# A hybrid decoder step on one core: PSUM banks and the token shift's way out of PSUM

## Chip, cores and metric

One core of a Trainium2 chip. The metric is the device time of one execution in microseconds, the median of the runs; lower is better. The kernel holds its numbers in fp32; a dense product is three passes of a rounded high part and a low part.

## What is computed

One layer over 1024 prompt tokens and 8 x 4 sample tokens (1056 columns in all), cut to what matters:

```
h = rmsnorm(x) ; z = h @ w_in                       # conv | r,k,v,lora | gates
xs = zr + (prev(zr) - zr) * mu                      # token shift: one token back
r, k, v, decay, alr, gout = from xs (three small lora products)
S_t = S_{t-1} diag(w_t) + (S_{t-1} a_t) b_t^T + v_t k_t^T ;  y_t = S_t r_t   # 16 heads, 64 x 64
y = groupnorm(y) ... ; ya = conv branch ; x += (sigmoid(zg0) * ya + sigmoid(zg1) * (y @ w_rw_out)) @ w_mix_out
x += (gelu(conv3(h2 @ w_up)[:half]) * conv3(...)[half:]) @ w_down ; rmsnorm
```

Outputs are the activations and the new conv, shift, wkv and ffn states.

## The kernel before

A dense product makes one tile of 128 output channels: `project_g` (L75) runs three blocks of 352 tokens, each 8 x 3 matmuls into one PSUM bank of the pool `pm` (tag mm, three banks), and hands each finished block to an eviction function. The weight tile comes by DMA, ScalarE rounds it (`whi`, L48), GpSimd makes the rest (`wlo`, L49).

The program has four parts. `load_in` and `norm_in` load and normalize. `mixer_a` does the conv tiles with their 31 taps on VectorE (L359), the lora products and the r, k, v tiles of the first two column groups. `mixer_b` runs the recurrence. `tail` does the merge, the output product and the feed-forward part with PSUM pools of its own.

In `mixer_b` the recurrence is cut into 16 pieces (4 groups of 4 heads, 4 quarters of the prompt), each of four chunks of 64 tokens. Nine generators, the streams, are recorded together with the dense tiles by `drive` (L701): a stream step that is due by an estimated tensor-engine clock is recorded, else one step of a dense tile, the fillers: first 18 tiles of r, k, v with their token shift, then 16 gate tiles, then 8 conv output tiles once the last chain is done. The streams are: `prep` (decays, normalized keys, the bonus; L885), `stage` (in-chunk products, L992, and a triangular solve of 31 steps on VectorE, L1026 to L1030, whose tiles go by DMA through DRAM), `combine` (L1061), `chain` (L1089: four steps, each a product from the state, a copy R0, a product, a scaled write of U, a product, the new state), `group_norm` (L1159), the samples' streams, the layer norm of the conv branch, and the shift output. They take working tiles from a pool of `T2N` = 12 buffers through a counter (`take`, L730).

From this record a scheduler sets the order on each engine; an engine then works strictly in it. PSUM has eight banks: three for dense tiles (tag mm), two that all streams share (tag w, `pw_tile`, L879), and one each for the chain (c), its output (y) and the solve (x). The same pools serve the first stages.

The token shift (`shifted`, L481) empties a dense bank in these steps: ScalarE writes (1 - mu) times the block (L490), VectorE adds mu times the block, one column to the right, reading PSUM (L492), adds the column kept from the block before (`bcol`, L494), keeps the last column (L496), and in the last block handles the samples and copies the shift state (`shcol`, L502, L503).

Of the kernel before, what the change touches and what calls it, by code (L numbers as in the profile page):

```python
# [7 lines left out]
F32 = mybir.dt.float32  # L8
# [3 lines left out]
ALU = mybir.AluOpType  # L12
# [19 lines left out]
class Net:  # L32
# [68 lines left out]
    def build(self):  # L101
        with ExitStack() as es:
# [6 lines left out]
            with ExitStack() as e1:  # L109
                self.rp = self.pool(e1, "wraw", 1)  # L110
                with ExitStack() as e:
                    self.pm = self.pool(e1, "pm", 3, space=PSUM)
                    self.pw = self.pool(e1, "pw", 2, space=PSUM)
                    xs, w0 = self.load_in(e)
                    self.norm_in(e, xs)
                with ExitStack() as e:
                    self.t4 = self.pool(e, "t4", 8)
                    self.mixer_a(w0)
                self.mixer_b()
# [132 lines left out]
    def mixer_a(self, w0):  # L252
# [5 lines left out]
        self.bcol = self.cp.tile([128, NSH, 2], F32, name="bcol")  # L258
# [128 lines left out]
    def ln_block(self, b):  # L387
# [14 lines left out]
        ps = self.pw_tile()  # L402
# [5 lines left out]
        ps = self.pw_tile()  # L408
# [72 lines left out]
    def shifted(self, w, j, out, m=128):  # L481
# [3 lines left out]
        bc = self.bcol[:m, j]  # L485
        add = lambda o, i: nc.vector.scalar_tensor_tensor(out=o, in0=i, scalar=mu, in1=o, op0=ALU.mult, op1=ALU.add)  # L486

        def ev(b, s, ps):
            t0 = b * BW
            nc.scalar.activation(out=out[:m, s], in_=ps, func=AF.Copy, scale=om)  # L490
            n = min(TP - t0, BW)
            add(out[:m, t0 + 1:t0 + n], ps[:, 0:n - 1])  # L492
            if b:
                add(out[:m, t0:t0 + 1], bc[:, b - 1:b])  # L494
            if n == BW:
                nc.vector.tensor_copy(out=bc[:, b:b + 1], in_=ps[:, n - 1:n])  # L496
            else:
                x = out[:m, TP:T].rearrange("p (b t) -> p b t", t=4)
                z = ps[:, n:BW].rearrange("p (b t) -> p b t", t=4)
                add(x[:, :, 1:4], z[:, :, 0:3])  # L500
                add(x[:, :, 0], self.shT[:m, j])
                nc.vector.tensor_copy(out=self.shcol[:m, j, 0:1], in_=ps[:, n - 1:n])  # L502
                nc.vector.tensor_copy(out=self.shcol[:m, j, 1:9], in_=z[:, :, 3])  # L503
# [165 lines left out]
    T2N = 12  # L669
# [157 lines left out]
    def s_shift(self):  # L827
# [3 lines left out]
        for g in range(7):  # L831
            yield from self.take(1)
            ps = self.pw_tile()
# [45 lines left out]
    def pw_tile(self):  # L879
        return self.pw.tile([128, 512], F32, tag="w", name="w")  # L880

# [3 lines left out]
    def prep(self, n):  # L885
# [79 lines left out]
        for u in ([slice(0, 1), slice(1, 2)] if smp else [slice(0, 2)]):  # L965
            ps = self.pw_tile()
# [715 lines left out]
```

## Time and profile before

| | us |
|---|---|
| median of 3 runs | 2560.39 (2559.02 to 2569.0) |
| profiled execution | 2538.03 |
| its span, first to last instruction | 2536.3 |
| tensor engine (PE) busy | 2367.6 |
| VectorE (DVE) busy | 1427.9 |
| ScalarE (ACT) busy | 918.7 |
| GpSimd (POOL) busy | 909.1 |

The engines' times overlap. Matmuls are pipelined, so a busy PE is not one at its peak. PEclk is the granted share of the tensor engine's full clock. PEld is the weight load, SP the engine that issues DMAs. A line such as L486 is a line of the kernel before; where a helper records an operation, the line is the helper's (L54 is every matmul, L61 every transpose of the recurrence). In the changed kernel the lines stand 4 to 17 further down.

### The profile page before, as it was taken

The numbers are of one execution on the slowest core, as the hardware profiler recorded it, in microseconds if no ns is written. First come the engines' busy times: TensorE is split into PE (matmuls) and PEld (weight loads), VectorE is DVE, ScalarE is ACT, GpSimd is POOL, SyncE is SP. The second block draws the span as 40 slices with busy tenths as digits, with TensorE's granted clock in tenths as the row PEclk, the third lists the DMA queues.
The fourth block names the chain that finished last, engine by engine and source line by source line (L and its number), as shares of the span: only waits on it lengthen the run. The fifth ranks groups of instructions, "written<-read, shape, count | busy, mean of one in ns | idle before, by whom it ended". The sixth has DMA issues, their size and how long they took to land.

```text
span 2536.3 us, 41660 instructions
## 1 busy us (share of the span) xinstructions
PE 2367.6 (93%) x16094; PEld 2140.9 (84%) x16094; DVE 1427.9 (56%) x3588; ACT 918.7 (36%) x1748; POOL 909.1 (36%) x879
## 2 busy tenths in 40 slices
PE   5889989999788799999989999999999999999998
PEld 4878888777676677777777899999999999999998
DVE  5799955586646674555464434465444534445345
ACT  4133433354244354454434322333222222223125
POOL 3332253244324443443333243433323323323333
PEclk9899987898688698999779999999999999999999
DMA  3223443243233333533323854431111111111111
GB/s 104 56 60 130 171 149 89 81 121 93 78 89 79 93 107 83 140 98 94 94 64 96 273 178 131 128 128 44 44 47 48 44 51 44 47 48 41 54 46 75
DMA packets 307640, 230.64 MB, mean 91 GB/s; under 512 B 90492, under 2 KB 287123, under 8 KB 306921
## 3 DMA queue, kind: packets, MB, share of 16 engines
q1 hardware_dynamic: 307185, 227.80, 31.1%
q8 instruction: 127, 2.08, 0.4%
q14 instruction: 72, 0.59, 0.1%
q0 software_dynamic: 256, 0.17, 0.0%
HBM read 157.45 MB, written 70.45 MB: 90 GB/s over the span
## 4 chain that ended last, share of the span: by engine, by line
PE 66%; DVE 7%; DMA 7%; POOL 3%; issue 2%; ACT 1%; SPq 1%; POOLq 0%; DVEq 0%; ACTq 0%
PE mm L54 52%; PE w L54 7%; DMA L<-dL 4%; PE c L54 2%; PE y L54 2%; PE w L61 2%; DVE tm L1028 1%; DVE x L1030 1%; DVE t L961 1%; DMA ga<-d_ga 0%; POOL BK L982 0%; POOL wlo L49 0%; POOL LQ L1011 0%; DVE lnQ L666 0%; DVE v L486 0%
## 5 line engine op out<-in xcount | busy, mean ns | idle before, releaser
L54 PE MATMUL mm<-hH,whi 128*128 128x352 f32 (+1 forms) x2568 | 887.6, 346 | 27.0 <-DVE bcol L496 11.2
L54 PE MATMUL mm<-hL,whi 128*128 128x352 f32 (+1 forms) x2568 | 866.2, 337 | 0.2 <-DVE hL L248 0.2
L54 PE MATMUL mm<-hH,wlo 128*128 128x352 f32 (+1 forms) x2568 | 862.7, 336 | 0.0
L54 PEld LDWEIGHTS mm<-hH,whi 128*128 128x128 f32 (+1 forms) x2568 | 499.4, 194 | 55.9 <-issue 14.1
L54 PEld LDWEIGHTS mm<-hL,whi 128*128 128x128 f32 (+1 forms) x2568 | 500.9, 195 | 11.2 <-DVE hL L248 0.5
L54 PEld LDWEIGHTS mm<-hH,wlo 128*128 128x128 f32 (+1 forms) x2568 | 500.6, 195 | 8.7 <-issue 0.2
L49 POOL TENSOR_TENSOR wlo<-wraw,whi 128x1024 fp32r<-128x1024 f32 (+2 forms) x123 | 292.5, 2378 | 462.0 <-ACT whi L48 427.9
L48 ACT ACTIVATE whi<-wraw 128x1024 fp32r<-128x1024 f32 (+2 forms) x123 | 126.0, 1025 | 366.8 <-PE mm L54 270.1
L1544 DVE SCALAR_TENSOR_TENSOR c<-u,par,c 128x1024 f32<-128x1024 f32 x96 | 167.0, 1739 | 55.6 <-ACT c L1540 55.6
L359 DVE SCALAR_TENSOR_TENSOR sg<-cu,par,sg 128x1024 f32<-128x1024 f32 x120 | 185.1, 1550 | 3.4 <-ACT sg L357 1.7
L1514 DVE TENSOR_TENSOR u<-mm,rs 128x352 f32<-128x352 f32 x144 | 73.2, 509 | 186.5 <-PE mm L54 186.3
L54 PE MATMUL mm<-fH,whi 128*128 128x352 f32 x504 | 163.4, 324 | 0.0
L1569 DVE TENSOR_TENSOR acc<-mm,acc 128x352 f32<-128x352 f32 x168 | 86.8, 523 | 135.0 <-PE mm L54 135.0
L54 PE MATMUL mm<-fH,wlo 128*128 128x352 f32 x504 | 162.7, 323 | 0.0
L54 PE MATMUL mm<-fL,whi 128*128 128x352 f32 x504 | 162.7, 323 | 0.0
L1028 DVE TENSOR_TENSOR tm<-L,x 128x60 f32<-128x60 f32 (+24 forms) x496 | 99.4, 200 | 79.7 <-DMA L<-dL 72.5
L1030 DVE TENSOR_TENSOR x<-x,tm 128x60 f32<-128x60 f32 (+24 forms) x496 | 105.0, 212 | 7.0
L1525 POOL COPY lr<-u 128x2 f32<-128x2 f32 x48 | 9.0, 187 | 276.3 <-DVE u L1514 267.6
L54 PE MATMUL w<-E,BK 64*128 64x128 f32 x512 | 90.7, 337 | 8.8 <-DVE tm L1028 3.4
L1011 POOL TENSOR_SCALAR_AFFINE_SELECT LQ<-LQ 64x512 f32<-64x512 f32 x64 | 44.1, 690 | 148.3 <-ACT LQ L1007 146.8
L54 PEld LDWEIGHTS mm<-fH,whi 128*128 128x128 f32 x504 | 94.8, 188 | 0.5
L54 PEld LDWEIGHTS mm<-fH,wlo 128*128 128x128 f32 x504 | 95.0, 188 | 0.0
(379 smaller groups left out, 3971.2 us busy)
## 6 DMA issues: line engine op xcount, KB each, us to landing
wraw<-w_in SPq DMA_DIRECT2D x50, 512.0 KB
wraw<-w_up SPq DMA_DIRECT2D x48, 512.0 KB
wraw<-w_down SPq DMA_DIRECT2D x32, 384.0 KB
L<-dL SPq DMA_DIRECT2D x16, 512.0 KB
d_alr<-la SPq DMA_DIRECT2D x8, 528.0 KB
d_cum<-lc SPq DMA_DIRECT2D x8, 528.0 KB
d_gout<-lg SPq DMA_DIRECT2D x8, 528.0 KB
d_k<-k SPq DMA_DIRECT2D x8, 528.0 KB
```

Source lines behind the costliest of these rows:

```text
L48: nc.scalar.activation(out=hi[:, :nk, :m], in_=raw[:, :nk, :m], func=AF.Copy)
L49: (lo_eng or nc.gpsimd).tensor_tensor(out=lo[:, :nk, :m], in0=raw[:, :nk, :m], in1=hi[:, :nk, :m].bitcast(F32), op=ALU.subtract)
L54: self.nc.tensor.matmul(out, l, r, start=start, stop=stop)
L61: self.nc.tensor.transpose(out, x, ident)
L359: nc.vector.scalar_tensor_tensor(out=c[:, 0:TP], in0=u[:, t:t + TP], scalar=self.col("conv_w", t * 4 + i), in1=c[:, 0:TP], op0=ALU.mult, o ...
L961: nc.vector.scalar_tensor_tensor(out=t1[:, u], in0=r[:, u], scalar=self.col("r_k", 2 * J + u), in1=km[:, u], op0=ALU.mult, op1=ALU.mult)
L1011: nc.gpsimd.affine_select(out=w, in_=w, pattern=[[0, 4], [1, 2], [1, 64]], compare_op=ALU.is_ge, fill=0.0, base=-1, channel_multiplier=-1)
L1028: nc.vector.tensor_tensor(out=tm[:, :a, :m], in0=L[:, s:s + 1, s + 1:32].to_broadcast([128, a, m]), in1=X[:, :a, s:s + 1].to_broadcast([12 ...
L1030: nc.vector.tensor_tensor(out=X[:, :a, s + 1:32], in0=X[:, :a, s + 1:32], in1=tm[:, :a, :m], op=ALU.add)
L1514: nc.vector.tensor_tensor(out=u[:, 2 + t0:2 + t0 + m], in0=p, in1=rs[:, t0:t0 + m], op=ALU.mult)
L1544: nc.vector.scalar_tensor_tensor(out=c[:, 0:TP], in0=u[:, t:t + TP], scalar=wt, in1=c[:, 0:TP], op0=ALU.mult, op1=ALU.add)
L1569: nc.vector.tensor_tensor(out=acc[i][:, s], in0=ps[:, :BW], in1=acc[i][:, s], op=ALU.add)
```

## The change

Four things. The first stages get PSUM pools of their own, five dense banks and three others, which end before the recurrence; the recurrence gets new pools: two dense banks (tag mm), two w, one each of u, c, y and x. The streams `prep` (its bonus), `group_norm`, the samples, the layer norm and the shift output take u instead of w; `stage`, `combine` and the norms of `prep` stay on w. The token shift leaves PSUM by ScalarE alone: it writes (1 - mu) times the block and, into a scratch tile z of a pool with two buffers, mu times the block; the shift state's copies are ScalarE's too; VectorE adds z one column to the right, and the add of a block is recorded only after the reads of the next one. The column kept between blocks goes. `T2N` is 11, and the product tile of the solve is packed into 96 columns.

```diff
-                    self.pm = self.pool(e1, "pm", 3, space=PSUM)
-                    self.pw = self.pool(e1, "pw", 2, space=PSUM)
+                    self.pm = self.pool(ep, "pm", 5, space=PSUM)
+                    self.pw = self.pool(ep, "pw", 3, space=PSUM)
...
+                    self.shp = self.pool(e1, "shift", 2)
...
+                self.pm = self.pool(e1, "pmb", 2, space=PSUM)
+                self.pw = self.pool(e1, "pwb", 2, space=PSUM)
                 self.mixer_b()
...
+        held = []
+        def add():
+            t0, n, z = held.pop()
+            nc.vector.tensor_tensor(out=out[:m, t0 + 1:t0 + 1 + n], in0=out[:m, t0 + 1:t0 + 1 + n], in1=z[:m, :n], op=ALU.add)
         def ev(b, s, ps):
             t0 = b * BW
+            n = min(TP - t0, BW)
             nc.scalar.activation(out=out[:m, s], in_=ps, func=AF.Copy, scale=om)
-            n = min(TP - t0, BW)
-            add(out[:m, t0 + 1:t0 + n], ps[:, 0:n - 1])
-            if b:
-                add(out[:m, t0:t0 + 1], bc[:, b - 1:b])
-            if n == BW:
-                nc.vector.tensor_copy(out=bc[:, b:b + 1], in_=ps[:, n - 1:n])
+            z = self.shp.tile([128, BW], F32, tag="z", name="z")
+            nc.scalar.activation(out=z[:m], in_=ps, func=AF.Copy, scale=mu)
+            if n < BW:
+                nc.scalar.copy(out=self.shcol[:m, j, 0:1], in_=ps[:, n - 1:n])
+                nc.scalar.copy(out=self.shcol[:m, j, 1:9], in_=ps[:, n:BW].rearrange("p (b t) -> p b t", t=4)[:, :, 3])
+            if held:
+                add()
+            if n == BW:
+                held.append((t0, n, z))
             else:
+                held.append((t0, n - 1, z))
+                add()
...
-    T2N = 12
+    T2N = 11
...
+    def pu_tile(self):
+        return self.pw.tile([128, 512], F32, tag="u", name="u", bufs=1)
...
-        tm = self.ln.tile([128, 8, 32], F32, tag="tm", name="tm")
+        tmf = self.ln.tile([128, 96], F32, tag="tm", name="tm")
...
+            tm = tmf[:, :a * m].rearrange("p (a t) -> p a t", t=m)
```

What the scheduler makes of it, at three places. First VectorE before, at the last block of a v tile in the recurrence; x and tm are the triangular solve, mm is the dense bank:

```order
L486 SCALAR_TENSOR_TENSOR v<-mm,par_180,v 128x319
L1028 TENSOR_TENSOR tm<-L,x 128x7x4
L486 SCALAR_TENSOR_TENSOR v<-bcol,par_180,v 128x1
L1030 TENSOR_TENSOR x<-x,tm 128x7x4
L486 SCALAR_TENSOR_TENSOR v<-mm,par_180,v 128x8x3
L1028 TENSOR_TENSOR tm<-L,x 128x8x3
L486 SCALAR_TENSOR_TENSOR v<-shT,par_180,v 128x8
L1030 TENSOR_TENSOR x<-x,tm 128x8x3
L502 COPY shcol<-mm 128x1
L503 COPY shcol<-mm 128x8
```

The bank is free after the last of these rows. In the changed kernel no row of VectorE reads a dense bank with the token shift.

Second, the changed kernel in the recurrence: ScalarE between the reads of two blocks (5609 is the first block of a v tile, 5498 the last of the r tile before it; the second read writes z), and behind it VectorE at the add that frees the buffer of z for it (5180 is the z two blocks earlier):

```order
L499 ACTIVATE v_5602<-mm_5609,omu_182 128x352
L1122 ACTIVATE SP_5228<-UV_4292,PC_3385 64x64 x2
L1023 ACTIVATE LQ_5248<-w_5270 64x4x64
L1024 ACTIVATE E1_5004<-w_5270 64x512
L408 ACTIVATE lnQ_5101<-lnC_5100 128x528
L501 ACTIVATE z_5582<-mm_5498,par0_180 128x352
```

```order
L1151 TENSOR_TENSOR UV_4292<-c_5283,nin_3466 64x2x64
L1045 TENSOR_TENSOR tm_4693<-L_4690,x_4692 128x49
L1151 TENSOR_TENSOR UV_4292<-c_5283,nin_3466 64x2x64
L1047 TENSOR_TENSOR x_4692<-x_4692,tm_4693 128x7x7
L493 TENSOR_TENSOR r_5106<-r_5106,z_5180 128x352
```

The first read of the later block has moved ahead of the second read of the earlier one. The add stands behind U of the chain (c 5283), whose product the tensor engine makes between the later block, 5609, and the first matmul that wants the earlier block's bank again.

Third, the tensor engine at the last two steps of the last chain (c, y: the chain's banks; mm: dense matmuls), before:

```order
L54 MATMUL c_13230<-UV_12454,E1_12003 64x64
L54 MATMUL y_12983<-UV_12454,E1_12003 64x64
L54 MATMUL mm_13999<-hH_63,wlo_13968 128x352
L54 MATMUL mm_13999<-hH_63,whi_13967 128x352
L54 MATMUL mm_13999<-hL_64,whi_13967 128x352
L54 MATMUL c_13252<-R0_13235,LQ_12211 64x64 x4
L54 MATMUL mm_13999<-hH_63,wlo_13968 128x352
```

and in the changed kernel, on to the first conv output tile (cs):

```order
L54 MATMUL c_13289<-UV_12512,E1_12003 64x64
L54 MATMUL y_13032<-UV_12512,E1_12003 64x64
L54 MATMUL c_13308<-R0_13294,LQ_12208 64x64 x4
L61 MATMUL u_13340<-ident_92,UX_13236 64x128 x4
L54 MATMUL y_13032<-UV_12512,LQ_12208 64x64
L54 MATMUL c_13324<-UV_12512,BK_12194 64x64 x4
L54 MATMUL y_13032<-UV_12512,LQ_12208 64x64 x3
L61 MATMUL u_13353<-ident_92,Sf_13329 64x128 x2
L61 MATMUL u_13417<-ident_92,UX_13236 64x128 x4
L61 MATMUL u_13517<-ident_92,Yev_13338 128x128 x4
L54 MATMUL mm_14216<-csH_13392,whi_14203 128x352
```

Before, 95 matmuls of gate tiles follow the last chain; in the changed kernel all 3672 matmuls of conv, r, k, v, lora and gate tiles stand ahead of its R0 products, and the conv output tiles follow.

## Rows read from the trace of the kernel before

**Rows 1.** The page: busy tenths and granted clock in 40 equal slices.

```profile
PE   5889989999788799999989999999999999999998
PEclk9899987898688698999779999999999999999999
```

**Rows 2.** Busy time by stage: stretch, us, PE, PEld, DVE, ACT, POOL, clock, DMA.

```profile
0.00:345.00 345.00, 297.17 (x1627) 261.81 (x1627) 276.65 (x363) 125.22 (x214) 102.97 (x99) 0.95 0.34 110
345.00:940.00 595.00, 519.05 (x3966) 433.80 (x3966) 381.95 (x1415) 259.35 (x582) 244.09 (x264) 0.82 0.35 94
940.00:1400.00 460.00, 429.50 (x3528) 343.73 (x3529) 247.40 (x951) 205.76 (x477) 175.21 (x175) 0.87 0.37 96
1470.00:2536.00 1066.00, 1058.33 (x6592) 1039.70 (x6590) 492.86 (x812) 303.72 (x443) 367.85 (x329) 1.00 0.23 68
```

**Rows 3.** PE's waits, 0 to 345 us: who, releaser, total us, times, longest.

```profile
PE mm L54 <- DVE bcol L496: 8.6, 4, 4.4
...
PE mm L54 <- DVE shcol L503: 1.4, 2, 1.0
```

**Rows 4.** PE's waits, 345 to 940 us.

```profile
PE w L54 <- DVE t L961: 12.2, 4, 3.6
PE mm L54 <- DVE shcol L503: 8.6, 2, 6.5
PE w L61 <- DVE x L1030: 7.6, 1, 7.6
PE w L54 <- DVE x L1030: 7.5, 2, 7.2
PE c L54 <- DVE R L1126: 6.6, 6, 4.9
PE w L54 <- DVE tm L1028: 6.5, 3, 3.4
...
PE mm L54 <- DVE bcol L496: 2.6, 2, 2.4
```

**Rows 5.** DVE's waits, 345 to 940 us.

```profile
DVE v L486 <- ACT v L490: 10.4, 7, 3.2
...
DVE k L486 <- ACT k L490: 8.9, 6, 4.2
```

**Rows 6.** DVE's groups by form, 345 to 940, busy us, mean ns; then L486's min/median/max.

```profile
L486 DVE SCALAR_TENSOR_TENSOR v<-bcol,par,v 128x1 f32<-128x1 f32 x12 | 7.1, 593 | 0.0
L486 DVE SCALAR_TENSOR_TENSOR v<-mm,par,v 128x351 f32<-128x351 f32 x12 | 6.9, 576 | 4.3 <-ACT v L490 4.3
...
L486 DVE SCALAR_TENSOR_TENSOR v<-bcol,par,v x16: 201/210/1551, 276.7 to 929.7; 128x1 f32<-128x1 f32 x16
...
L496 DVE COPY bcol<-mm x54: 107/150/159, 118.4 to 926.1; 128x1 f32<-128x1 f32 x52, 32x1 f32<-32x1 f32 x2
```

**Rows 7.** Line 1208, a subtraction with both inputs in SBUF: min/median/max ns.

```profile
L1208 DVE TENSOR_TENSOR hL<-hL,hH x8: 1247/1256/1452, 1418.1 to 1442.6; 128x1056 fp32r<-128x1056 f32 x8
```

**Rows 8.** ACT's groups, 345 to 940 us.

```profile
L490 ACT ACTIVATE v<-mm,omu 128x352 f32<-128x352 f32 x18 | 9.9, 552 | 24.6 <-PE mm L54 24.4
```

**Rows 9.** PE's waits, 940 to 1400 us.

```profile
PE mm L54 <- ACT gt L454: 3.5, 1, 3.5
```

**Rows 10.** PE's waits, 1400 to 1470 us.

```profile
PE mm L54 <- DVE ga L441: 4.9, 3, 3.6
```

**Rows 11.** The chain that ended last, a dense stretch: start, us, what.

```profile
1612.58 11.70 PE mm L54 x72
```

**Rows 12.** Timeline of PE and DVE around the last chain's end; one row of the chain of waits.

```profile
1393.72 0.45 PE L54 MATMUL c<-UV,E 128*64 128x64 f32 x8
...
1408.68 0.66 PE L61 MATMUL w<-ident,Yev 128*128 128x128 f32 x4 [1.13 <-POOL Yev L1223]
...
1397.21 1.20 DVE L1145 SCALAR_TENSOR_TENSOR Sf<-c,PC,SP 64x64 f32<-64x64 f32 x4 [1.15 <-PE c L54]
...
1394.95 0.38 PE c L54 x8
```

**Rows 13.** Line 1028, 345 to 940 us: min/median/max ns.

```profile
L1028 DVE TENSOR_TENSOR tm<-L,x x280: 151/204/234, 390.5 to 939.7; 128x60 f32<-128x60 f32 x12, 128x54 f32<-128x54 f32 x10, 128x66 f32<-128x66 f32 x9, 128x28 f32<-128x28 f32 x8
```

More of the change, by code (lines that the diff above doesn't have):

```diff
@@ L257, in mixer_a @@
         self.shT = self.cp.tile([128, NSH, 8], F32, name="shT")
-        self.bcol = self.cp.tile([128, NSH, 2], F32, name="bcol")
         self.done = set()
@@ L484, in shifted @@
         om, mu = self.omu[:m, j:j + 1], self.par["mu"][:m, j:j + 1]
[L485 to L486 removed]
+        held = []
+        def add():
+            t0, n, z = held.pop()
+            nc.vector.tensor_tensor(out=out[:m, t0 + 1:t0 + 1 + n], in0=out[:m, t0 + 1:t0 + 1 + n], in1=z[:m, :n], op=ALU.add)
         def ev(b, s, ps):
             t0 = b * BW
+            n = min(TP - t0, BW)
             nc.scalar.activation(out=out[:m, s], in_=ps, func=AF.Copy, scale=om)
[L491 to L494 removed]
+            z = self.shp.tile([128, BW], F32, tag="z", name="z")
[5 more added lines that the diff above has]
+                add()
             if n == BW:
[L496 removed]
+                held.append((t0, n, z))
             else:
+                held.append((t0, n - 1, z))
+                add()
                 x = out[:m, TP:T].rearrange("p (b t) -> p b t", t=4)
[L499 to L503, printed above, removed]
+                nc.vector.tensor_tensor(out=x[:, :, 1:4], in0=x[:, :, 1:4],
+                                        in1=z[:m, n:BW].rearrange("p (b t) -> p b t", t=4)[:, :, 0:3], op=ALU.add)
+                nc.vector.scalar_tensor_tensor(out=x[:, :, 0], in0=self.shT[:m, j], scalar=mu, in1=x[:, :, 0], op0=ALU.mult, op1=ALU.add)
         yield from self.project_g(w, (self.hH, self.hL), 8, ev, m)
@@ L1027, in stage @@
             a, m = s // 4 + 1, 31 - s
-            nc.vector.tensor_tensor(out=tm[:, :a, :m], in0=L[:, s:s + 1, s + 1:32].to_broadcast([128, a, m]),
+            tm = tmf[:, :a * m].rearrange("p (a t) -> p a t", t=m)
+            nc.vector.tensor_tensor(out=tm, in0=L[:, s:s + 1, s + 1:32].to_broadcast([128, a, m]),
                                     in1=X[:, :a, s:s + 1].to_broadcast([128, a, m]), op=ALU.mult)
-            nc.vector.tensor_tensor(out=X[:, :a, s + 1:32], in0=X[:, :a, s + 1:32], in1=tm[:, :a, :m], op=ALU.add)
+            nc.vector.tensor_tensor(out=X[:, :a, s + 1:32], in0=X[:, :a, s + 1:32], in1=tm, op=ALU.add)
         Xs = self.ln.tile([128, 8, 32], F32, tag="X", name="X")
@@ L1237, in samples_in @@
         yield 4000
-        ps = self.pw_tile()
+        ps = self.pu_tile()
         for g in range(2):
@@ L1266, in samples_in @@
         yield 2000
-        G = self.pw_tile()
+        G = self.pu_tile()
         for x in range(2):
```

37 lines of the change are left out of this document (19 added, 18 removed).

## Prediction

> **What bounds the kernel now.** I read the page first: the matmul row is busy for 93% of the span, and its clock row is full from slice 23 on, but between 6 and 9 tenths before that [rows 1]. Then the table by stage [rows 2]. The last 1066 us have the tensor engine busy for 1058 at a clock of 1.00: nothing that the diff touches runs there, and nothing is to be gained. The first stages (345 us) leave 48 us idle, the recurrence beside the token-shift tiles (345 to 940) leaves 76 and runs at 0.82 of the clock, the recurrence beside the gate tiles (940 to 1400) leaves 30 at 0.87. So what can move is idle time and clock before 1400 us. The tensor engine takes its instructions in order, so one wait stops dense tiles and streams alike. The waits by stage [rows 3, 4] name VectorE nearly every time: it is late, not the tensor engine. Two kinds must be kept apart. A dense matmul that waits for the token shift (bcol, shcol) waits for its PSUM bank. A transpose of state rows that waits for a step of the triangular solve has only loaded rows as input, so it waits for a bank too. The others wait for data.
>
> **The change part by part.** Durations are those of the profiled execution, 2538.0 us; the median of the three timed runs is 2560.4, so the sum is made against 2538.0 and its difference set on 2560.4.
>
> *First stages, five dense banks and three for the others.* The two waits for the shift there, 8.6 and 1.4 us [rows 3], go: a bank is asked for again four groups later. VectorE is busy for 277 of the 345 us [rows 2] and may take over as the bound, so I count **-8** (ends 0 and -10).
>
> *Shift on ScalarE, streams with a bank of their own, beside the recurrence.* The waits for shcol and bcol, 8.6 and 2.6 us, and the 7.6 us of the state transposes [rows 4] go: **-18.8** (ends -11 and -18.8). The first order block shows the worst of them: the two copies that free the bank stand behind the steps of the solve.
>
> *VectorE's relief.* Today VectorE, which also goes in order, stands still until ScalarE has read the bank: 10.4 and 8.9 us [rows 5]. The held add ends that. Per tile the wide operations cost 3 x 0.576 and the boundary ones 2 x 0.593 [rows 6], some 2.9 us. The new add, two SBUF inputs of 352 columns, is not in this trace; a third of the 1.256 us of the 1056-column subtraction, 0.42, is the lower bound [rows 7]. The boundary operations, which take two SBUF inputs today, range from 0.20 to 1.55 us for one column with a mean of 0.593: something holds them up 0.38 us on average [rows 6]. With that the add costs 0.80. I take 0.80, three per tile, 2.4 us. So 0.5 us are saved in each of 18 tiles, 9 us, or 30 us with adds of 0.42. The Trainium skill (SBUF — State Buffer, Who interferes with whom) says that a VectorE instruction with two SBUF inputs contends with a GpSimd instruction that reads SBUF, while one with a single SBUF input does not. By that rule the change moves the wide operations, which had one input in PSUM, into the contention; the spread of the boundary rows agrees, and 0.80 rather than 0.42 is what the rule gives. With the 19.3 us of standing still VectorE has some 28 us less in a stretch where it is busy for 382. The waits for its late results there are 12.2, 7.5, 6.6 and 6.5 us [rows 4]. I take a third of these 32.8: **-10** (ends 0 and -25).
>
> *The price: two dense banks, and ScalarE reading twice.* A second read costs 0.552 us [rows 8]; 18 x 3 of them on an engine that is busy for 259 of 595 us [rows 2] cost nothing by themselves. But the scratch tile of a second read has two buffers, and an add that VectorE has not reached holds ScalarE, and with it the bank. The order has three places (the second pair of blocks is one) where ScalarE's second read needs an add that stands on VectorE behind chain work which the tensor engine does just before it wants the bank again. Each is a wait between 1.1 us (two reads) and 6.5, the longest for a shift bank today [rows 4]; at 3.8 that is 11.4. The gate's 3.5 us [rows 9] come again: **+15** in all (ends +3 and +30). The conv tiles at the end wait 4.9 us for the product that empties their bank [rows 10]; a group of 12 matmuls lasts 12 x 11.70/72 = 1.95 us [rows 11], and one bank less makes two such waits that much longer: **+4**.
>
> *One stream buffer less (11 for 12).* No row shows it; the order does. Prep, stage and combine fall behind the dense tiles, and the third pair of blocks shows where this ends: today the last chain has dense matmuls between its steps and 95 behind it; afterwards all dense tiles of the gates stand ahead of it and its four steps stand bare. A step takes 4.7 us, from 1393.72 to 1398.41 [rows 12]; the tensor engine's own part is three groups of 0.38 and about as much for the outputs, an estimate of 2.1, so four bare steps add 4 x 2.6 = 10.4 us. Then the normed rows are transposed 10.3 us after the chain, of which 1.1 is idle today [rows 12]: 9.1 more. Together **+19.5** (ends +12 and +27, the latter with the slow clock). The 95 matmuls, 15.4 us at the rate of [rows 11], now stand earlier, in stretches that have 106 us of idle time, and may fill half of it each: **-8** (ends 0 and -15.4).
>
> *Clock.* From the gate stretch to the shift stretch the idle share goes from 6.6 to 12.8% and the lost clock from 13 to 18% [rows 2], 0.8 for 1. The terms above take 22 us of idle time out of 1055, 2.1%; that is 1.7% of clock, 18 us, of which small matmuls see little: **-9** (ends 0 and -18).
>
> *At nothing:* the compact product tile of the solve (same operations and sizes), the other tile pools, the shcol copies (0.15 us each, now on ScalarE). No transfer is added, and none changes its place on SyncE's or GpSimd's queue but by the drift above.
>
> The sum: -8 -18.8 -10 +15 +4 +19.5 -8 -9 = **-15.3 us**: 2522.7 for the profiled execution, **2545.1** on the median.
>
> **The rivals.** *(a) The bare end is paid and the waits only move.* Most idle time in [rows 4] is for data, and the streams are as long as before. Then the relief, the clock term and the filling vanish and the new waits eat the old: -8 -18.8 +15 +4 +19.5 = +11.7, about 2570 with everything, 2560 if half of the relief stays. For it: the waits for data are twice those for banks. Against: VectorE does lose work.
>
> *(b) Slower: ScalarE is caught on the scratch tiles.* The place is the shift stretch: 54 groups in 595 us, one every 11 us. The point from which it decides is a VectorE queue that needs longer than a group to come to a held add; a solve without a break is 62 operations of 0.204, 12.6 us [rows 13], a little over it. Some nine solves lie in the stretch (280 steps, 31 each). If each catches one second read for 12.6 + 1.1 - 11 = 2.7 us, that is 24.3 in place of the 11.4 above, and since ScalarE's other stream work queues behind it, relief, filling and clock are gone: -8 -18.8 +24.3 +3.5 +4 +19.5 = +24.5, 2585. Against: on VectorE the solve's steps are interleaved with other work, as the first block shows, so an add need not wait for its end.
>
> *(c) Faster still: the waits were most of the clock.* New waits at their lower end (+3), filling at its upper (-15.4), clock at -18: -8 -18.8 -10 +3 +4 +19.5 -15.4 -18 = -44, 2517. For it: the low slices of the clock lie where the longest waits are. Against: the longest waits for data stay.
>
> That the change does not do what it says is excluded for the shift by the order, where VectorE no longer reads a dense bank. The Trainium skill (ScalarE: Activation LUTs, Rules for kernel authors) wants add and mul on VectorE; here both engines take the same for a read from PSUM, 0.552 and 0.576 us [rows 6, 8], so by the row nothing is lost, and by the rule each second read would be dear, which the ends of the price hold.
>
> **How the numbers follow.** About 0.5% (12.8 us) is what a measurement can tell from no change. Forecast 0.40, (a) 0.25, (b) 0.20, (c) 0.15. The forecast lies near the bound: 0.27 of it faster, 0.13 the same. Of (a) I give 0.02 to either side. Faster: 0.27 + 0.15 + 0.02 = 0.44. Slower: 0.20 + 0.02 = 0.22. Same: 0.13 + 0.21 = 0.34. The range: from below (c), 2503 (relief also at -25), to (b), 2585; that leaves out about a tenth on each side. The forecast's own range is 2530 to 2558.
>
> **What would show it.** No tensor-engine wait on the shift in the first stages, and the matmuls of the token shift waiting, if at all, for ScalarE; VectorE's standstill for ScalarE's read near zero; adds of about 0.8 us; the tensor engine idle for some 20 us around the last chain, before the conv tiles, at a lower clock; the last 1066 us as they are. Wrong I would be if the idle time between 345 and 1400 us stays at 106 us or grows (then (a) or (b), told apart by whether ScalarE waits for the adds), or if the bare end costs nothing because the chain comes earlier than the order lets it seem.

## The result, and the profile after

The changed kernel takes **2596.19 us** (median of 4, 2582.42 to 2601.96) against 2563.56 (median of 4): ratio 1.0139, 95% interval 1.0100 to 1.0178. It is **slower by 1.4%**, 11 us above the upper end of the forecast's range and on the other side of its sign. The profiled execution took 2601.96 us (span 2600.3, mean clock 0.909); the profile of before, 2538.03 us at 0.926, lies at the lower edge of its own runs, so the two profiles are 64 us apart where the medians are 33 apart. Sizes are therefore read from the ratios; what the profiles show of stages holds for these two executions.

The page of the changed kernel, busy tenths and granted clock in 40 slices of 65 us:

```profile
PE   6989989988898789998989799999999999999998
PEclk9989978886798877897889799999999999999999
```

Compared with [rows 1], the same picture: a full tail, and before it a clock between 6 and 9 tenths, now for longer. Busy time by stage of the changed kernel (stretch, us, PE, PEld, DVE, ACT, POOL, clock, DMA), cut at the 1369th dense matmul (recurrence begins), the 2665th (all r, k, v tiles done; I call the part between the shift stretch), the first conv output tile, and the tail:

```profile
0.00:374.50 374.50, 321.87 (x1749) 286.25 (x1750) 298.80 (x341) 153.49 (x296) 138.41 (x128) 0.91 0.34 112
374.50:992.20 617.70, 539.53 (x3949) 444.69 (x3948) 365.41 (x1306) 280.77 (x656) 235.66 (x248) 0.80 0.32 89
992.20:1478.30 486.10, 444.74 (x3513) 349.64 (x3512) 249.00 (x939) 207.40 (x472) 166.36 (x165) 0.85 0.35 99
1478.30:1534.10 55.80, 51.20 (x299) 49.40 (x297) 19.36 (x29) 13.88 (x19) 12.67 (x9) 0.95 0.71 238
1534.10:2600.30 1066.20, 1058.70 (x6591) 1040.05 (x6591) 491.55 (x812) 304.20 (x444) 368.17 (x329) 1.00 0.22 68
```

The kernel before, cut at the same dense matmuls:

```profile
0.00:374.50 374.50, 321.32 (x1741) 283.61 (x1742) 299.66 (x402) 137.85 (x238) 124.51 (x125) 0.93 0.35 111
374.50:975.90 601.40, 526.20 (x4058) 438.42 (x4057) 378.13 (x1468) 258.61 (x586) 236.88 (x253) 0.82 0.35 92
975.90:1414.70 438.80, 411.77 (x3410) 330.60 (x3410) 234.42 (x876) 202.82 (x464) 165.36 (x166) 0.89 0.40 104
```

The tail is the same (1066 us). The first stages end at the same 374.5 us: no gain shows there. The shift stretch is 16 us longer, the rest up to the first conv tile 47 us. How that comes about: I add up two things in each trace, the time in which neither a matmul nor a weight load ran, and the time at which the granted clock stood at its lower level (1.2 of 2.4 GHz). Up to the first conv tile idle time goes from 154 to 172 us, time at half clock from 365 to 462. Half of the latter is lost work: 17 + 97/2 = 66 us, against 63.5 by the times of the first conv tile. **Between these two executions three quarters of the difference are clock, one quarter is idle time.** The bare end, which the table below explains, holds 12 of the 17 us and 32 of the 97. For the medians the share of the clock is smaller, because the profile of before had a high clock among its runs. Time x clock, which counts a half-clock microsecond as half, is 2347 us on average over the 94 runs of the kernel before that stand beside the experiments (mean time 2559) and 2365 over the 4 of the changed kernel (mean time 2594): **of 35 us, 18 are more time as counted at the full clock and 17, about half, are the lower clock.** In f0, the changed kernel again, it is 17 and 23 us against the runs beside it.

The tensor engine's waits in the changed kernel, 0 to 345 us:

```profile
PE mm L54 <- ACT whi L48: 9.5, 1, 9.5
PE mm L54 <- POOL wlo L49: 6.5, 2, 4.9
...
PE mm L54 <- ACT shcol L504: 2.0, 1, 2.0
```

and 345 to 940 us:

```profile
PE mm L54 <- ACT shcol L504: 13.9, 3, 12.0
PE u L54 <- DVE t L977: 12.7, 2, 7.2
PE w L54 <- DVE x L1047: 8.8, 1, 8.8
```

VectorE's bcol and shcol of [rows 3, 4] are gone, as they had to be. In their place come waits for ScalarE's reads of a bank, one of them 12.0 us long. ScalarE and VectorE there, and the matmul that waits:

```profile
886.00 1.09 ACT L972 ACTIVATE alr<-alr,oka,par 128x256 f32<-128x256 f32 x2 [2.43 <-DVE kn L948]
887.64 0.38 ACT L1049 ACTIVATE X<-x 128x256 f32<-128x256 f32 x1 [0.55 <-DVE x L1047]
887.92 0.55 ACT L499 ACTIVATE v<-mm,omu 128x352 f32<-128x352 f32 x1
894.19 0.55 ACT L501 ACTIVATE z<-mm,par 128x352 f32<-128x352 f32 x1 [5.72 <-DVE r L493]
```

```profile
890.74 1.70 DVE L997 TENSOR_TENSOR E<-r,P 64x512 f32<-64x512 f32 x1
892.47 1.25 DVE L678 SCALAR_TENSOR_TENSOR lnQ<-lnQ 128x132 f32<-128x132 f32 x1
893.64 0.52 DVE L493 TENSOR_TENSOR r<-r,z 128x352 f32<-128x352 f32 x1
```

```profile
882.60 0.32 PE L54 MATMUL mm<-hH,wlo 128*128 128x352 f32 x1
894.91 0.66 PE L54 MATMUL mm<-hH,whi 128*128 128x352 f32 x1 [11.99 <-ACT shcol L504]
```

ScalarE has read the next tile's first block (L499, the moved-up read of the second order block) and then stands 5.72 us, because the scratch tile's add is late on VectorE, behind stage and layer-norm work. The scratch tile is thus about half of this stop: in the 5 us before, ScalarE did the streams' work and waited 2.43 and 0.55 us for VectorE's `kn` and the solve. The bank stays full, and the matmuls resume at 894.91 at twice their time (0.66 for 0.32): the granted clock stands at its lower level from 886.5 to 900.2 us.

### The profile page after: what moved, and what is told of

Same layout as the page of the kernel before. It is cut to its first block, busy times and chain, and to the rows that moved or that the text cites. A ratio compares the mean times of both kernels' runs of the same rounds, so it can differ in the third digit from the quotient of the medians.

```text
span 2600.3 us, 41630 instructions
## 1 busy us (share of the span) xinstructions
PE 2416.0 (93%) x16094; PEld 2170.0 (83%) x16094; DVE 1424.1 (55%) x3426; ACT 959.7 (37%) x1883; POOL 921.3 (35%) x879
## 4 chain that ended last, share of the span: by engine, by line
PE 51%; DMA 2%; DVE 1%; POOL 1%; ACT 1%; issue 1%; SPq 0%; ACTq 0%; POOLq 0%; DVEq 0%
PE mm L54 44%; PE w L54 2%; DMA L<-dL 1%; PE c L54 1%; PE y L54 1%; PE u L54 1%; PE u L61 1%; DMA ga<-d_ga 0%; PE w L61 0%; PE w L1440 0%; PE w L1525 0%; DMA d_ma<-ga 0%; POOL y L1211 0%; PE w L1546 0%; DVE hL L1225 0%
## 5 line engine op out<-in xcount | busy, mean ns | idle before, releaser
L54 PE MATMUL w<-E,BK 64*128 64x128 f32 x512 | 111.3, 368 | 6.4 <-POOL BK L999 4.5
L54 PEld LDWEIGHTS w<-E,BK 64*128 64x128 f32 x512 | 86.7, 249 | 26.7 <-issue 8.0
L1122 ACT ACTIVATE SP<-UV,PC 64x64 f32<-64x64 f32 x192 | 64.9, 343 | 108.1 <-DVE UV L1162 98.6
```

What stands on the lines that cost most here:

```text
L54: self.nc.tensor.matmul(out, l, r, start=start, stop=stop)
L1122: nc.scalar.activation(out=at(SP, u, x), in_=src(x)[:, u], func=AF.Copy, scale=PC[hs[x], 4 * u + c:4 * u + c + 1])
```

## Experiments

Theories, as they stood when they were named. **D**: the missing twelfth buffer lets the streams fall behind and end bare. **B**: the recurrence's third dense bank is what is missed. **H**: holding the adds catches ScalarE on the scratch tiles. **S**: the streams' own bank bunches them. **Cover**: what counts is how the streams lie among the dense tiles. The kernel before was measured beside each group of runs; ratios are to that. Two columns come from the traces: the shift stretch (its 1296 dense matmuls, and what streams ran between them), and the bare end, from the last gate matmul to the first conv tile, in which only streams run.

| run | median us | ratio (95%) | shift stretch us | bare end us |
|---|---|---|---|---|
| before (profile) | 2552 to 2565 | 1 | 601 | 0 |
| changed | 2596.2 | 1.014 (1.010 to 1.018) | 618 | 37 |
| f0 changed again | 2602.9 | 1.015 (1.009 to 1.021) | 624 | 37 |
| a1 pools only | 2547.7 | 0.996 (0.992 to 0.999) | 597 | 0 |
| a2 11 buffers only | 2575.8 | 1.006 (1.002 to 1.010) | 589 | 43 |
| a3 banks, no shift | 2587.6 | 1.012 (1.007 to 1.016) | 679 | 0 |
| a4 12 buffers, one z | 2628.7 | 1.026 (1.020 to 1.032) | 705 | 0 |
| b1 two dense | 2586.1 | 1.012 (1.006 to 1.019) | 686 | 0 |
| b2 two dense, three w | 2579.2 | 1.009 (1.006 to 1.013) | 687 | 0 |
| b3 shift only, 11 | 2574.0 | 1.006 (1.003 to 1.009) | 556 | 97 |
| b4 three dense, no u, 11 | 2589.8 | 1.012 (1.006 to 1.018) | 557 | 85 |
| c1 adds at once | 2558.3 | 0.999 (0.996 to 1.003) | 572 | 13 |
| c2 three dense, one z, 12 | 2559.8 | 0.997 (0.993 to 1.001) | 587 | 0 |
| d1 dummies at the end | 2606.9 | 1.016 (1.009 to 1.023) | 638 | 39 |
| f1 three dense, at once, 11 | 2605.3 | 1.017 (1.008 to 1.025) | 553 | 109 |
| f2 three dense, at once, 12 | 2545.7 | 0.992 (0.988 to 0.996) | 599 | 0 |
| f3 two dense, at once, 12 | 2576.8 | 1.004 (1.000 to 1.008) | 614 | 0 |
| g1 held, four z | 2610.7 | 1.022 (1.016 to 1.029) | 565 | 54 |
| g2 held, two z, bf16 | 2613.1 | 1.025 (1.017 to 1.033) | 621 | 38 |
| h1 = f1 paced | 2550.3 | 1.000 (0.997 to 1.003) | 596 | 17 |

The last two columns are of one execution each. The changed kernel's order was profiled three times (changed, f0, g2) and its shift stretch took 618 to 624 us. The trace of f2 is of the longest of its ten runs (2565.68 us).

### The parts one by one

a1, to the kernel before:

```diff
-                    self.pm = self.pool(e1, "pm", 3, space=PSUM)
-                    self.pw = self.pool(e1, "pw", 2, space=PSUM)
+                    self.pm = self.pool(ep, "pm", 5, space=PSUM)
+                    self.pw = self.pool(ep, "pw", 3, space=PSUM)
...
+                self.pm = self.pool(e1, "pmb", 3, space=PSUM)
+                self.pw = self.pool(e1, "pwb", 2, space=PSUM)
```

> The kernel before with the first stages' own pools alone (five dense banks, three others; the recurrence keeps three dense and two w). Theory D (the missing working buffer makes the streams late, they end bare, and the clock is lost there) expects no loss: 2556 to 2564, the first 1368 dense matmuls done 0 to 10 us earlier. Rival B (the recurrence's two dense banks and the held adds cost it) expects the same, 2556 to 2564. A third account, that the five banks shift the first stages' work so that VectorE or the weights become the bound there, expects 2565 to 2575 and the 1368th dense matmul no earlier than before.

Faster, 0.45% or 11.5 us, a little below the expected interval; the recurrence begins at 362 us instead of 374.5. In the changed kernel it begins at 374.5. Over all profiles, the four with these pools and VectorE's shift (a1, a3, b1, b2) begin it at 361 to 371 us, 364 on average, the thirteen with ScalarE's shift at 366 to 378, 372 on average, and before and a2 at 374.5 and 376.5. So the shift on ScalarE seems to take some 7 of the 11 us back; one order alone (changed, f0, g2) varies by 7.

a2, to the kernel before:

```diff
-    T2N = 12
+    T2N = 11
```

> The kernel before with 11 working buffers for the streams in place of 12, nothing else. Theory D expects most of the loss of the change here: 2580 to 2595, with half-clock time and idle time around the last chain as in the changed kernel. Rival B expects 2558 to 2566, since no bank has changed.

Slower by 0.6%, 15 us: between the two expectations. D is a part of it, less than half, and it looks as D says: a bare end of 43 us.

a3, to the changed kernel, with `shifted` of the kernel before in the place of its own:

```diff
-                    self.shp = self.pool(e1, "shift", 2)
...
-    T2N = 11
+    T2N = 12
```

> The changed kernel with VectorE's token shift of the kernel before and 12 buffers: what is left of the change are the pools of the first stages, two dense banks and the streams' own bank. Theory D expects the loss gone: 2540 to 2562, the last chain with dense matmuls between its steps and some 400 behind it. Rival B, in the form that two dense banks cost it, expects 2580 to 2600; in the form that the held adds cost it, about 2560.

No bare end and still slower by 1.2%: D alone falls, and B in its first form holds. What is left of the change there are the pools, which gain, and the bank that moved from the dense tiles to the streams.

a4, to the changed kernel:

```diff
-                    self.shp = self.pool(e1, "shift", 2)
+                    self.shp = self.pool(e1, "shift", 1)
...
-    T2N = 11
+    T2N = 12
```

> The changed kernel with 12 working buffers, which fit if the shift's scratch tile z has one buffer in place of two. Theory D expects most of the loss gone, 2550 to 2570, although ScalarE now waits for the add of each block before the next second read. Rival B expects it as slow as the changed kernel or slower, 2595 to 2625, with longer waits of dense matmuls for ScalarE.

The slowest of all, a little above what B expected. The pair with c2 below tells why.

### The banks

b1 and b2, to a1 (the w line in b2 only):

```diff
-                self.pm = self.pool(e1, "pmb", 3, space=PSUM)
+                self.pm = self.pool(e1, "pmb", 2, space=PSUM)
-                self.pw = self.pool(e1, "pwb", 2, space=PSUM)
+                self.pw = self.pool(e1, "pwb", 3, space=PSUM)
```

> The kernel with the first stages' pools alone, and in the recurrence two dense banks in place of three; the freed bank is left empty, VectorE keeps the token shift, 12 buffers. Theory B (what costs is the third dense bank that is gone) expects 2570 to 2590 against 2548 with three, with more waits of dense matmuls for shcol, bcol and gt and more time at half clock between 375 and 1480 us. Theory S (what costs is the streams' own bank, which lets them bunch) expects 2545 to 2560. Theory H (what costs is the shift on ScalarE with its held adds) expects 2545 to 2560 too.

> As the run with two dense banks, but the freed bank goes to the streams as a third shared one (w) rather than one of their own. Theory B expects about the time of two dense banks with none given, less up to 8 us: 2565 to 2590. Theory S expects the loss here, 2575 to 2595, and none with the bank left empty. Theory H expects 2540 to 2560.

**The third dense bank is worth 1.7%, 43 us** (0.996 to 1.012), with the token shift as it was; given to the streams as a third w it returns 0.3%, less than the intervals can tell. B holds, and S has no support: the loss is there with the freed bank empty, and a3, where the streams have that bank to themselves, is no slower (1.012). The dense matmuls' waits of [rows 4] grow. First with three banks (a1), then with two (b1), to the end of the gates:

```profile
PE mm L54 <- DVE bcol L499: 4.2, 1, 4.2
PE mm L54 <- DVE shcol L506: 3.4, 2, 2.1
```

```profile
PE mm L54 <- DVE shcol L506: 14.1, 3, 8.1
...
PE mm L54 <- DVE x L1033: 5.7, 2, 2.9
...
PE mm L54 <- DVE rt L667: 3.3, 1, 3.3
```

These waits are the smaller part. Up to the first conv tile idle time goes from 149 to 167 us and time at half clock from 393 to 437: 17 + 44/2 = 39 us, of 38 by the times of that tile.

b3, to the kernel before, with `shifted` and the packed product tile of the changed one:

```diff
+                self.shp = self.pool(e1, "shift", 2)
...
-    T2N = 12
+    T2N = 11
```

b4, to the changed kernel:

```diff
-                self.pm = self.pool(e1, "pmb", 2, space=PSUM)
+                self.pm = self.pool(e1, "pmb", 3, space=PSUM)
...
-        return self.pw.tile([128, 512], F32, tag="u", name="u", bufs=1)
+        return self.pw.tile([128, 512], F32, tag="w", name="w")
```

> The kernel before with the token shift on ScalarE with held adds and 11 buffers; pools as before (three dense, two w, the same in the first stages). 11 buffers alone gave 2575.8. Theory B expects the shift to gain what VectorE no longer waits for: 2555 to 2575. Theory H expects 2590 to 2610. Theory S expects 2565 to 2580.

> The changed kernel with the streams' own bank given back: three dense banks, two w that all streams share. Theory B expects most of the loss gone but for the 11 buffers: 2555 to 2575. Theory S expects the same, 2555 to 2575. Theory H expects 2590 to 2605, no better than the changed kernel.

b3 is as slow as 11 buffers alone (1.0062 and 1.0060): the shift on ScalarE gains nothing net, and with three banks the held adds do not cost what H expected. Its shift stretch is the quick one that I had forecast, 556 us for 589 in a2, but its end is bare for 97 us for 43. b4 is a miss for B, and its time is at the edge of H's interval: three banks, a quick shift stretch, and all of it given back in a bare end of 85 us. This is where the second mechanism showed: in these orders the dense tiles stand further ahead, and the streams are left over.

### Holding the adds

c1, to the changed kernel (`z` is as wide as before; ScalarE also copies the last column):

```diff
+            bc = self.bcol[:m, j]
             if n < BW:
...
-            if held:
-                add()
-            if n == BW:
-                held.append((t0, n, z))
             else:
-                held.append((t0, n - 1, z))
-                add()
+                nc.scalar.copy(out=bc[:, b:b + 1], in_=ps[:, n - 1:n])
+            nc.vector.tensor_tensor(out=out[:m, t0 + 1:t0 + n], in0=out[:m, t0 + 1:t0 + n], in1=z[:m, :n - 1], op=ALU.add)
+            if b:
+                nc.vector.scalar_tensor_tensor(out=out[:m, t0:t0 + 1], in0=bc[:, b - 1:b], scalar=mu, in1=out[:m, t0:t0 + 1], op0=ALU.mult, op1=ALU.add)
```

> The changed kernel, but VectorE's add of a block is recorded at once and not behind the reads of the next block; ScalarE copies the last column to a small tile and VectorE adds it with the next block. Two dense banks, u and 11 buffers stay. Theory H (holding the adds catches ScalarE on the scratch tiles, 56.4 us of ScalarE's waits in 18 pieces, and through it the dense bank) expects the dense matmuls' waits of 24.4 us between the 1368th dense matmul and the tail to fall below 14 and the time to 2565 to 2585. Theory B (two banks leave no slack for whatever reads them late) expects the waits to stay above 18 us and 2588 to 2602.

**The whole loss is gone** (0.999), by more than H had expected, though two dense banks, u and 11 buffers stay. The shift stretch, with 3924 matmul records for 3949, so nearly the same mix of work:

```profile
371.30:943.20 571.90, 510.36 (x3924) 421.40 (x3923) 371.71 (x1319) 280.72 (x687) 229.91 (x242) 0.85 0.34 94
```

46 us shorter than the changed kernel's 617.70 at a clock of 0.80; idle time there falls from 78 to 61 us, time at half clock from 249 to 167. The bare end is 13 us for 37, of which the conv tiles give 9 back (64.5 us for 55.2, to their last matmul). But H's own sign was missed: the waits of dense matmuls for their bank did not fall (24.4 to 27.0 us, with the conv tiles). So the edit is shown to undo the loss; that it does so through the stops at the bank is not shown. How long ScalarE's second read waited for adds, over the whole run, in the changed kernel and in c1:

```profile
  ACT z L501: 56.4, 18
```

```profile
  ACT z L502: 22.7, 7
```

c2, to b4, so that it differs from a4 in the banks alone:

```diff
-                    self.shp = self.pool(e1, "shift", 2)
+                    self.shp = self.pool(e1, "shift", 1)
...
-    T2N = 11
+    T2N = 12
```

> The first stages' pools and the shift on ScalarE with held adds, three dense banks and two w (no u), 12 buffers, one scratch tile z. It differs from the run with twelve buffers and one z only in the banks. Theory B expects the dense matmuls' waits of 57.4 us there to fall to 5 to 20 and the time to 2540 to 2562, as good as the first stages' pools alone. Theory H (ScalarE is caught on the scratch tiles whatever the banks) expects 2595 or more. The account by cover (what counts is how evenly the streams lie over the dense tiles) expects 2540 to 2565, because the last chain is no longer bare.

0.997: B and cover are right. Who waits for the z operations in a4 and in c2 (us, times; the two PE rows are the same stops, seen by the weight load and by the matmul):

```profile
  ACT z L501: 103.1, 45
  PEld mm L54: 39.9, 5
  PE mm L54: 38.5, 5
```

```profile
  ACT z L501: 116.5, 45
  PEld mm L54: 14.0, 3
  PE mm L54: 13.3, 2
```

ScalarE is caught as often and longer in c2, yet the tensor engine stops a third as long: **with three banks ScalarE may be late, with two it may not**. That is 0.997 against 1.026.

f0, f1, f2 and f3 stand side by side: the changed kernel again, and the edit of c1 (adds at once) made in b4 (f1), in c2 (f2) and in a4 (f3).

> The changed kernel, measured again beside the next three. If the difference between it and the run with adds at once is real, it stands at 2585 to 2605; if it was chance between measurements, at 2560 to 2575.

> The first stages' pools, shift on ScalarE, three dense banks, no u, 11 buffers (2589.8 with held adds), now with the adds at once. In its order the last two chains and part of the one before them have no dense matmul left. Theory H (holding the adds is the loss) expects 2550 to 2570. The account by cover (a bare end costs the latency of its steps) expects no gain: 2585 to 2610.

> The first stages' pools, shift on ScalarE with adds at once, three dense banks, no u, 12 buffers, one scratch tile (2559.8 with held adds). Theory H expects a gain, 2540 to 2553. The account by cover expects what the held adds gave there, 2550 to 2565, since three banks hide ScalarE's waits and the last chain is covered in both.

> The changed kernel with 12 buffers and one scratch tile (2628.7 with held adds, 57.4 us of dense matmuls' waits), now with the adds at once. Theory H expects the waits below 30 us and the time at 2555 to 2580. Theory B (two dense banks cost it however they are read) expects 2590 or more.

In f2 and f3 the tile of kept columns is smaller; the operations are those of c1. The loss repeats (1.015). Adds at once gain 2.2% with two banks (a4 to f3), 0.5% with three (c2 to f2), nothing where the end is bare (b4 to f1, where H expected 2550 to 2570 and cover was right). Read the other way, the third bank is worth 2.9% with held adds (a4 to c2) and 1.2% with adds at once (f3 to f2): neither price stands by itself. And the twelfth buffer, with one z less, takes the bare end and the loss away where there are three banks: 1.5% from b4 to c2, 2.5% from f1 to f2. **f2 is the fastest of all, 0.992 (0.988 to 0.996)**: pools of their own for the first stages, shift on ScalarE with adds at once, three dense banks, no u, 12 buffers. Over a1, the pools alone, it is 0.4% ahead, within what the intervals leave open.

g1 and g2 ask by which link the held adds cost, to the changed kernel (four buffers in g1 only):

```diff
-            z = self.shp.tile([128, BW], F32, tag="z", name="z")
+            z = self.shp.tile([128, BW], mybir.dt.bfloat16, tag="z", name="z")
...
-                    self.shp = self.pool(e1, "shift", 2)
+                    self.shp = self.pool(e1, "shift", 4)
```

> The changed kernel with held adds and the scratch tile z in bf16 with four buffers in the same space (the token shift is rounded there, so the output differs from the reference by that). ScalarE's waits for the adds, 56.4 us, should fall below 15. The account by the catch expects 2555 to 2575. The account by the late adds expects 2590 to 2605. In the order the dense tiles move ahead and the whole last chain stands bare, so the account by cover expects 2590 to 2610 too, with the half-clock time at the end of the recurrence.

> As before, z in bf16 with two buffers: the order is that of the changed kernel, row for row on the tensor engine. All accounts expect the changed kernel's time, 2588 to 2605; if the type itself matters (shorter adds), up to 10 us less.

g1's ScalarE waits 5.5 us for adds in place of 56.4, and it is slow all the same: the 2555 to 2575 that the account by the catch expected are missed. It doesn't settle the link: its shift stretch is 565 us for g2's 621, so the relief is there, but its end is bare for 54 us for 38, and the gates' stretch takes 500 us for 444. That stretch in g1, then in g2 (columns as in the tables by stage):

```profile
931.30:1430.80 499.50, 472.13 (x3276) 371.96 (x3275) 236.12 (x924) 191.78 (x444) 169.00 (x171) 0.75 0.31 86
```

```profile
988.10:1431.70 443.60, 416.16 (x3294) 330.74 (x3294) 227.06 (x888) 189.93 (x440) 160.07 (x159) 0.88 0.34 92
```

The idle time is the same, 27 us in each, with nearly the same number of matmuls; the clock is 0.75 for 0.88, 246 us at half clock for 106. So here the clock alone takes back what the shift stretch had gained, and why it stays low is not shown. g2, the control, missed its expectation too: same order as the changed kernel, but 2613 where 2588 to 2605 was expected; its interval overlaps that of f0.

### The end

d1 records 96 matmuls more behind the last gate tile of the changed kernel:

```diff
                 if not gates:
                     self.done.add("gates")
+                    for i in range(16):
+                        ps = self.pm.tile([128, 512], F32, tag="mm", name="mm")
+                        for k in range(6):
+                            self.mm(ps[:, 0:256], self.hH[:, 6 + k % 2, 896:1024], self.hH[:, 6 + k % 2, 768:1024], k == 0, k == 5)
+                            yield 0
```

> The changed kernel with 96 matmuls more (256 columns, one pass each, results not read) recorded behind the last gate tile; the scheduler puts them between the steps of the last chain, where no dense matmul is left. At the full clock they take 96 x 256/2.4 GHz = 10.2 us. If the bare end costs its clock, the 37.6 us at half clock there shrink by more than half and the time falls or stays in spite of more work: 2575 to 2596. If the bare end costs only the latency of its steps, the clock does not matter there and the time is 2594 to 2608.

2606.9: by the expectation latency, not clock, though the whole time could not be told from f0. The end itself tells more. From the last gate matmul to the first conv tile it takes 39.4 us with them and 37.1 without, although the time at half clock there falls from 32 to 5 us: the higher clock does not shorten that end, unless by less than the 96 matmuls cost.

h1, to f1:

```diff
-    TINV = 29750
+    TINV = 32000
```

> The kernel with the first stages' pools, three dense banks, adds at once and 11 buffers (2605.3), with one constant changed: a combine is recorded 32000 units of the recorder's clock after its stage instead of 29750. In its order two of the three bare chains get dense matmuls again: the last chain's products lie between dense matmuls 3528 and 3672. The account by cover expects 2550 to 2580 and the waits for the combine's products (w from D and LQ, 50.9 us) to fall below 30. If the place of the streams is not the cause, 2595 to 2612.

**One pacing constant takes 1.6% away** (1.017 to 1.000): the bare end falls from 109 to 17 us, while the shift stretch grows from 553 to 596. The wait for the combine's first input in the last 170 us before the conv tiles of f1, then of h1 (total us, times, longest):

```profile
PE w L54 <- DVE D L1086: 20.3, 3, 12.4
```

```profile
PE w L54 <- DVE D L1086: 5.3, 1, 5.3
```

D is the solve's result, which the combine multiplies. At a bare end the solve's own latency is on the path, with no dense matmul beside it. The combine's waits over the whole recurrence went from 50.9 to 33.7 us, a little above the 30 expected.

## Why the prediction was wrong

Two causes carry the loss, and each was undone alone in some kernel: **two dense banks behind an engine that can be late** (a1 to b1, a4 to c2, changed to c1), and **streams left over at the end** (b4 to c2, f1 to f2, f1 to h1; a2 by itself). The changed kernel has both, 618 and 37 us in the table. By what steps the first becomes time is shown in part only.

- *First stages, -8.* Right alone: a1 gives 11.5 us. In the sum most of it went: with the shift on ScalarE the recurrence begins some 7 us later on average. ScalarE's 38.3 us of waiting for adds before 345 us (10 waits, where five banks rotate) and the 9.5 us for whi above are what stands there; that they are the cause was not tried alone.
- *The waits of [rows 3, 4], -18.8.* They went, but beside the recurrence 13.9 + 1.3 us for ScalarE came where 8.6 + 2.6 for VectorE had been, and 2.0 before it.
- *VectorE's relief, -10.* The relief is there in part. In the shift stretch, with the same dense matmuls, VectorE is busy for 365 us for 378, 13 less where I had said 9; part of that is stream work that now lies elsewhere (1306 instructions for 1468). But its standstill for ScalarE's read between 345 and 940 us is 9.9 us (7.5 + 2.4), not near zero, for 19.3 before. In b3 it is worth nothing net, because the end gives it back. The add was near its value: 51 of them between 345 and 940 us take 35.4 us, 0.70 each, against 0.80.
- *Two dense banks and two reads, +15.* **This is the step that failed.** I priced the missing bank by direct stops alone, three places at 3.8 us and the gate's 3.5. One stop was 12.0 us where I took 6.5 for the longest, but in sum the direct stops came out near what I had said: beside the recurrence ScalarE was caught 8 times for 18 us (the other 10 of its 18 waits lie in the first stages), and the dense matmuls waited 24.4 us for a bank from there to the tail, for 19.6 before. The price is more than these stops: 43 us for the bank alone with VectorE's shift and no scratch tile (a1 to b1), 31 with ScalarE's and adds at once (f2 to f3), and some 38 for holding the adds in the changed kernel (to c1), where the direct stops did not shrink at all. These do not add up: with 11 buffers the third bank by itself gains next to nothing (changed to b4, 1.014 and 1.012), because the end takes it back. The upper end of +30 was too low as well.
- *The conv tiles, +4, and the filling, -8.* Neither is seen. The tensor engine idles 4.5 us in the conv tiles for 4.9 before, and in the shift and gate stretches 107 us for 102.
- *One buffer less, +19.5.* Right in size: a2 measures 15 us, within +12 to +27. But the bare steps are hardly idle, as I had put it (12 of the end's 37 us): the chain's small matmuls fill them at half clock, as this piece of the changed kernel's end shows.

```profile
1456.20 0.69 PE L54 MATMUL c<-R,LQ 64*64 64x64 f32 x8 [0.18 <-DVE R L1143]
...
1462.34 0.69 PE L54 MATMUL c<-R,LQ 64*64 64x64 f32 x8 [0.19 <-DVE R L1143]
...
1477.49 1.11 PE L61 MATMUL u<-ident,Yev 128*128 128x128 f32 x4 [8.50 <-POOL Yev L1240]
1478.27 0.66 PE L54 MATMUL mm<-csH,whi 128*128 128x352 f32 x1
```

The last three steps begin 6.2, 4.7 and 6.1 us after the one before them, against 4.7 in [rows 12]; then the normed rows are waited for 8.5 us, against 1.13 there; that part was foreseen.

- *Clock, -9.* Wrong in sign and size. The idle time grew by 17 us in place of falling by 22, and it did not cost 0.8 for 1: time at half clock grew by 97 us, 48 us of work, in these two executions, and by the runs' means the clock costs 17 us. Nor do small matmuls see little of it: the eight `c<-R,LQ` above take 0.69 us, 0.45 in the kernel before at 1394.88. Over 19 profiles (d1 left out) time at half clock grows by 2.4 us with each idle us, with a wide scatter (correlation 0.68): g1 has no more idle time than the kernel before (156 and 154 us) and 507 us at half clock to 365.
- *The sign of being wrong* came as named: the idle time between 345 and 1400 us stayed (107.4 us for 106.5), and ScalarE waits for the adds, which points at (b).
- *Rival (b)* had the sign, and its 2585 came nearest, in part by luck. That ScalarE is caught on the scratch tiles is shown by the timeline and, as a price with two banks, by a4 against c2; that it is the loss of the changed kernel is not, for g1 nearly took the catches away and stayed slow. Its point, a whole solve ahead of the add, is not what the stop shows: stage and layer-norm work stood there. *Rival (a)* described b3: the waits only move.

For the add I had taken 0.80, with 0.42 as the bound from a row; 0.70 lies nearer the former. By the Trainium skill (SBUF — State Buffer, Who interferes with whom) a VectorE instruction with two SBUF inputs contends with a GpSimd instruction that reads SBUF. A long add in the changed kernel, and GpSimd beside it:

```profile
604.45 2.68 DVE L493 TENSOR_TENSOR v<-v,z 128x319 f32<-128x319 f32 x1
```

```profile
604.40 2.38 POOL L49 TENSOR_TENSOR wlo<-wraw,whi 128x1024 fp32r<-128x1024 f32 x1
```

The add ends 0.35 us after GpSimd's 2.38 us. Of the 81 adds the 45 with less than a tenth of their time beside a GpSimd instruction take 0.50 us on average, none over 0.53; the 28 with more than 0.6 take 1.23. This trace agrees with the rule, but the term was not what failed.

What stays open: why c1 gains 46 us in the shift stretch when the direct stops for a bank did not shrink, whether by ScalarE's queue, by the adds that no longer come together on VectorE, or by the clock's own course. Each edit of buffers or adds also moves the streams in the order, g1 among them. And f1 to h1 changes waits and cover together.

## What to carry to other kernels

Price a buffer by who empties it: here the PSUM bank taken from the dense tiles cost 1.2% where its reader's adds were recorded at once, 1.7% where VectorE read it, and 2.9% where the reader could be caught in turn, by a scratch tile whose consumer is late. A sum over the stops that an order shows is not that price. Where work streams are woven into dense work by a planner, relief for the dense side can leave the streams over, so read the end of the order and pace again before judging an edit: here one constant was worth as much as the whole change. And do not count idle time at its length alone: here about half of the loss was clock, and g1 lost clock without more idle time.

## Not expected of the hardware

The spread between runs of one kernel follows the granted clock: beside a1 the kernel before ran between 2541.39 us (clock 0.924) and 2575.85 us (0.911), and over its 94 runs beside the experiments the correlation of time and clock is -0.94. And a kernel can be faster with no less work at full clock: time x clock is 2365 us on average for the changed kernel's 4 runs and 2369 for c1's 10, but the clock is 0.912 against 0.926, which is the whole difference between them. Against the kernel before (2347 us, 0.917), c1 thus still carries some 22 us more, and makes them up by its clock.
